# S5 read-out tables of layer 0: formed beside the attention, kept in DRAM, and fetched by the read-out

## The chip, the core and the metric

The kernel runs on one core of a Trainium2 chip, as one launch. The metric is the device time of one execution in microseconds, as the median of several executions. TensorE does the matmuls, VectorE and ScalarE the elementwise work, GpSimd (POOL) the S5 scan and a few stores, and SyncE (SP) issues nearly all DMAs, in order, from one queue.

## The reference, cut to what matters

The model is a two-layer diffusion backbone over 256 latent and 256 context tokens of width 1024. Each layer projects the modulated tokens once and feeds three mixers beside each other, whose results are gated, summed and projected out, followed by an FFN. All matmuls of the projections run as three fp32r products (high and low halves), so their cost is three times a plain one.

The mixer that the change touches is the S5 branch: 32 groups of 16 channels, 64 complex states per group, two directions, a linear recurrence over the tokens.

```python
def s5_readout(x_re, x_im, c_re, c_im):
    return (jnp.einsum('ghp,blgp->blgh', c_re, x_re)
            - jnp.einsum('ghp,blgp->blgh', c_im, x_im))
...
        y_lat = y_lat + seq_order(s5_readout(xl_re, xl_im, c_re[dirn], c_im[dirn]), rev)
...
    g = jax.nn.gelu(y)
    return g * jax.nn.sigmoid(g @ w_glu + b_glu)
```

The kernel does the recurrence over chunks of eight tokens. The states at the chunk edges come from a scan on GpSimd. Inside a chunk each output is the sum of a part from the chunk's own inputs (the direct weights, 8 x 8 taps of 16 x 16) and of a part from the states at its two edges, times C times the powers of the transition (the read-out tables). Tables and direct weights depend on the parameters alone, not on the tokens.

## The kernel before, in words

`layer` strings stages together with `weave(main, (side, rate), ...)`: for each step of the main generator, so many steps of each side generator are issued; what is left of the sides follows at the end. The order on each engine is then written by a planner that runs the whole program in a model of its timeline, so instructions may be taken ahead of others on their engine; the order of the source gives their priority. On the chip each engine, and SyncE's queue, takes its instructions in the order written.

Layer 0 runs these stages around the change: `m_na(l, 0)` (keys, values and queries of half the heads, beside the S5 input side); `m_na(l, 1)` beside `s5_scan` on GpSimd, `attn(l, 0)` and five steps of `ada` (modulation weights of later stages); `gates(l, 0)`, eight projections of 128 gate columns, beside `attn(l, 1)` and `ada`; `gates(l, 2)` beside the S5 read-out `s5_out` and `ada`; then `branch_mm(l, 2)`, the matmuls of the attention branch, and `m_ret` beside `s5_glu`. Each of the attention's halves holds six softmax passes (two head pairs, three passes each).

`s5_out` works through four blocks of eight groups. In layer 0 it forms for each block, in place:

- `s5_g`: fetches C (lines 665 to 667, three DMAs), flips a sign on ScalarE (line 1110), and forms the 128 x 2304 tables `gb` by `_prods`, six products on VectorE of 128 x 1152 (lines 737 to 739, two directions).
- `s5_kwin`: 32 matmuls of the tables with BB, the input-side weights (line 1146), two copies (lines 1150, 1151), three small additions (lines 1152, 1155), and a store of the 128 x 480 direct weights to `kws` in DRAM (line 1159).
- `s5_t`: reads them back as the tile `T`, shifted so that each tap finds its place (four DMAs, line 1133).
- 48 matmuls per token stream, 96 in layer 0 (line 1211), of inputs with `T` and of states with `gb`; then GELU, a transpose and a split (lines 1218 to 1225).

Layer 1 does it otherwise. Its tables and direct weights are formed by `s5_kwins(1)` in the FFN of layer 0, the tables are stored to `gsp` (line 1169), and `s5_out` fetches them by `s5_back` (line 1124 for the tables, line 1133 for `T`), one block ahead of their use.

A weight is fetched by `wraw` (line 373) into one of four slots of 512 KB, then split into a high half by ScalarE (line 383) and a low half by VectorE (line 384), three deep. Lines 389 to 391 are the three products of `mm3`. A projection of 512 tokens by 128 columns has 24 matmuls of 512 columns. Line 517 is `ada`, and lines 1656 and 1659 end a gate projection (tanh, and a store to `tgs` by GpSimd's queue). Scratch buffers come from one pool, `F`, handed out round robin, so that a buffer's memory is taken again after the pool has turned once.

Of the kernel before, what the change touches and what calls it, by code (L numbers as in the profile page):

```python
# [9 lines left out]
F32 = mybir.dt.float32  # L10
# [8 lines left out]
P = 128  # L19
NL = 2  # L20
# [183 lines left out]
def weave(main, *sides):  # L204

    acc = [0.0] * len(sides)
    live = [True] * len(sides)

    def step(i):
        try:  # L210
            next(sides[i][0])
        except StopIteration:
            live[i] = False

    for _ in main:
        for i, (_, each) in enumerate(sides):
            acc[i] += each
            while live[i] and acc[i] >= 1.0:
                acc[i] -= 1.0
                step(i)  # L220
    while any(live):
        for i in range(len(sides)):
            if live[i]:
                step(i)
# [6 lines left out]
def chain(*gens):  # L231
    for g in gens:
        yield from g


class Net:
# [10 lines left out]
    def run(self, stack):  # L247
        tc, nc = self.tc, self.nc
# [4 lines left out]
        dr = stack.enter_context(tc.tile_pool(name="dr", bufs=1, space=DRAM))  # L253
# [3 lines left out]
        self.kws = dr.tile([NL * 4, P, 480], F32, name="kws")  # L257
        self.tgs = dr.tile([24, P, 512], F32, name="tgs")
        self.xsp = dr.tile([P, 4096], F32, name="xsp")
        self.gsp = dr.tile([4, P, 2304], F32, name="gsp")  # L260
        self.F = Arena(fa, NF, "F")
        self.R = Arena(ra, NR, "R")
        F, R = self.F, self.R
# [624 lines left out]
    def layer(self, l):  # L888
        nc, F = self.nc, self.F
        last = l == NL - 1  # L890
        n = self.nt = 256 if last else 512
        self.n0 = 512 - n
        na = [None, None]
        self.yna = self.yslot[0]
        if l == 0:
            self.ug = F.alloc(2048, "ug", top=True)
            mu = self.m_u(l)
            los = []
            for qt in range(1, 4):
                next(mu)  # L900
                self.ada2(0, qt)
                next(mu)
                los += self.modulate(0, 0, [0, 1], self.rb0, 0, range(qt * 2, qt * 2 + 2))
            self.pfree(self.rb0)
            self.s5_prep_small(self.s5in, los[9])
            for _ in mu:
                pass
            with self.tc.issue_after(self.wdma.ins):
                nc.sync.dma_start(self.xsp, self.xb.ap)
            self.xb.free()  # L910
            b2 = self.s5_tables(0)
            ada = self.ada(0, (2, 3, 4, 5))
            self.adas = ada
            self.X = F.alloc(4 * 66 * 16, "X", top=True)
            e_in = chain(*(g for blk in range(4) for g in (self.s5_e(0, b2, blk), self.s5_in(0, blk))))
            weave(self.m_na(l, 0, na), (e_in, 3))
            self.log_gamma(self.s5in[:, 192:208])
            weave(self.m_na(l, 1, na), (self.s5_scan(l), 18), (self.attn(l, 0, na), 4), (self.take(ada, 5), 1))
            weave(self.gates(l, 0, None), (self.attn(l, 1, na), 1.6), (self.take(ada, 5), 0.5))
            self.swap.free()  # L920
            weave(self.gates(l, 2, None), (self.s5_out(l, self.yslot[1]), 2), (self.take(ada, 5), 0.5))
            self.ug.free()
            self.X.free()
            self.m = F.alloc(8 * n, "m", top=True)
            for _ in self.branch_mm(l, 2, None, self.yna, first=True):
                pass
            weave(self.m_ret(l), (self.s5_glu(l, self.yslot[1], self.yslot[0]), 0.8), (self.ret_decay(l), 0.75))
            self.yret = self.yslot[1]
            tg = F.alloc(8 * n, "tg", top=True)
            weave(chain(self.branch_mm(l, 0, None, self.yslot[0]), self.gates(l, 1, tg)), (self.retention(l), 2))  # L930
            self.x_alloc()
            nc.sync.dma_start(self.xb.ap, self.xsp)
            for _ in self.branch_mm(l, 1, tg, self.yret, final=True):
                pass
        else:
            self.norm(l, 0, [2, 3])
            nc.sync.dma_start(self.xsp, self.xb.ap)
            self.xb.free()
            for _ in self.e_left:
                pass  # L940
            for b in self.tabs[l]:
                b.free()
            self.ug = F.alloc(2048, "ug", top=True)
            self.X = F.alloc(4 * 66 * 16, "X", top=True)
            kpre = self.pair([("ws", l, O_NK + m * 128) for m in range(2)])
            for _ in self.m_u(l):
                pass
            weave(self.m_na(l, 0, na, kpre), (chain(*(self.s5_in(l, blk) for blk in range(4)), self.s5_scan(l)), 20))
            ada = self.adas
            weave(self.m_na(l, 1, na), (self.attn(l, 0, na), 2.5))  # L950
            self.yret = self.yslot[1]
            weave(self.m_ret(l), (self.attn(l, 1, na), 1.2), (self.ret_decay(l), 0.75))
            self.swap.free()
            self.m = F.alloc(8 * n, "m", top=True)
            weave(self.branch(l, 2, self.yna, 0), (self.retention(l), 2.5))
            tg = F.alloc(8 * n, "tg", top=True)
            ys5 = self.yslot[0][:, 1024:]
            weave(chain(self.branch(l, 1, self.yret, 1), self.gates(l, 0, tg)),
                  (chain(self.s5_out(l, self.yslot[0]), self.s5_glu(l, self.yslot[0], ys5)), 1))
            self.ug.free()  # L960
            self.X.free()
            self.x_alloc()
            nc.sync.dma_start(self.xb.ap, self.xsp)
            for _ in self.branch_mm(l, 0, tg, ys5, final=True):
                pass
# [151 lines left out]
    def g_view(gb):  # L1117
        return gb.ap.rearrange("p (q r d n) -> p q r d n", q=4, r=2, d=2)

    def s5_back(self, blk):  # L1120

        nc = self.nc
        gb, T = self.F.alloc(2304, "g"), self.F.alloc(1024, "T")
        nc.sync.dma_start(gb.ap, self.gsp[blk])
        self.s5_t(1, blk, T)
        return gb, T

    def s5_t(self, l, blk, T):
# [33 lines left out]
    def s5_kwins(self, l):  # L1162

        nc = self.nc
        for blk in range(4):
            gb, gv = self.s5_g(l, blk)
            yield
            self.s5_kwin(l, blk, gv)
            nc.sync.dma_start(self.gsp[blk], gb.ap)
            gb.free()  # L1170
            yield

    def s5_out(self, l, ysl):
# [6 lines left out]
            return mk(self.X.ap, (r * 132 + d * 67 + st * 33) * 16 + gp, [[16, 32]])  # L1180

        gh, gl = self.halves(ysl)
        back = self.s5_back(0) if last else None
        for blk in range(4):
            if last:
                gb, T = back
                gv = self.g_view(gb)
                back = self.s5_back(blk + 1) if blk < 3 else None
                yield
            else:  # L1190
                gb, gv = self.s5_g(l, blk)
                yield
                self.s5_kwin(l, blk, gv)
                yield
                T = F.alloc(1024, "T")
                self.s5_t(l, blk, T)
                yield
            Tv = T.ap.rearrange("p (q r n) -> p q r n", q=4, r=2)

            n = self.nt  # L1200
# [626 lines left out]
```

## Time and profile before

| | |
|---|---|
| median of three runs | 1575.58 us (1569.61 to 1577.39) |
| the profiled execution | 1571.81 us, span 1570.0 us, mean granted clock 0.979 |
| TensorE busy | 1494.5 us, 95% |
| VectorE busy | 988.2 us, 63% |
| ScalarE busy | 632.2 us, 40% |
| GpSimd busy | 204.2 us, 13% |
| DMA | 245.92 MB, mean 157 GB/s |

The busy shares are means over stages with different limits. A stage is read from its own stretch: how long each engine was busy in it, the clock that TensorE was granted there (1.00 is 2.4 GHz, 0.50 is 1.2 GHz), the mean busy share of the 16 DMA engines and what they moved. In a row of the windows the engines stand in the order PE, PEld (weight loads), VectorE, ScalarE, GpSimd. In a row of the timeline, the bracket at the end is the idle time just before the instruction and what ended it.

### The profile page before, as it was taken

What the parts mean: (1) busy time and instruction counts of PE and PEld (TensorE: products, weight loads), DVE (VectorE), ACT (ScalarE), POOL (GpSimd) and SP (SyncE); (2) the same over time, 40 slices, a digit from 0 to 9 for tenths busy, and PEclk for the clock granted to TensorE, in tenths of its full rate; (3) what the DMA queues carried; (4) which work ended last, traced back from release to release, by engine and by line L of the source; (5) the groups of instructions that cost most, each with busy time, mean ns of one, the idle gap of its engine ahead of it and who ended that gap; (6) DMA issues with size and microseconds to landing.
All of it is one profiled execution on the core that took longest, in us unless ns stands there. A gap on an engine that the chain in (4) does not pass through costs nothing.

```text
span 1570.0 us, 25507 instructions
## 1 busy us (share of the span) xinstructions
PE 1494.5 (95%) x10066; PEld 1270.5 (81%) x10066; DVE 988.2 (63%) x1799; ACT 632.2 (40%) x1139; POOL 204.2 (13%) x541
## 2 busy tenths in 40 slices
PE   7979999969999999999999999999998999999997
PEld 5767677747887888887887788898677999899997
DVE  6784444466446588587699973732654776766566
ACT  4545544223422344332333322544644345443443
POOL 0004983000000000000000000006981000000000
PEclk9989999979999999999999999999999999999999
DMA  9413346654433333454566662422224786655553
GB/s 370 150 61 104 126 141 192 191 160 146 130 103 94 133 95 121 161 187 135 172 220 197 215 192 66 168 102 79 93 91 112 235 298 193 211 176 188 175 186 97
DMA packets 78585, 245.92 MB, mean 157 GB/s; under 512 B 9088, under 2 KB 22912, under 8 KB 76672
## 3 DMA queue, kind: packets, MB, share of 16 engines
q1 hardware_dynamic: 76864, 237.92, 46.3%
q0 software_dynamic: 1600, 6.36, 1.4%
q8 instruction: 79, 1.29, 0.3%
q14 instruction: 42, 0.34, 0.1%
HBM read 225.96 MB, written 16.12 MB: 154 GB/s over the span
## 4 chain that ended last, share of the span: by engine, by line
PE 88%; DMA 4%; DVE 4%; ACT 2%; issue 1%; SPq 0%; POOL 0%; POOLq 0%; DVEq 0%; ACTq 0%
PE psall L389 23%; PE psall L391 22%; PE psall L390 22%; PE psall L862 3%; PE psall L864 3%; PE psall L863 3%; DMA fa<-in_wst_dram 2%; PE psall L1049 1%; PE psall L1363 1%; PE psall L1398 1%; PE psall L1370 1%; PE psall L517 1%; PE psall L1211 1%; PE psall L754 1%; PE psall L1570 1%
## 5 line engine op out<-in xcount | busy, mean ns | idle before, releaser
L389 PE MATMUL psall<-ra 128*128 128x256 f32 (+1 forms) x2122 | 713.7, 341 | 10.5 <-DVE fa L1152 3.7
L391 PE MATMUL psall<-ra 128*128 128x256 f32 (+1 forms) x2122 | 708.9, 337 | 1.8 <-DVE ra L384 1.8
L390 PE MATMUL psall<-ra 128*128 128x256 f32 (+1 forms) x2122 | 710.5, 336 | 0.0
L384 DVE TENSOR_TENSOR ra<-fa,ra 128x1024 fp32r<-128x1024 f32 (+1 forms) x284 | 343.5, 1212 | 297.8 <-ACT ra L383 282.8
L383 ACT CAST ra<-fa 128x1024 fp32r<-128x1024 f32 (+1 forms) x284 | 293.7, 1037 | 564.4 <-PE psall L390 327.7
L389 PEld LDWEIGHTS psall<-ra 128*128 128x128 f32 x2122 | 402.9, 191 | 68.4 <-issue 11.7
L391 PEld LDWEIGHTS psall<-ra 128*128 128x128 f32 x2122 | 405.0, 191 | 45.4 <-issue 3.1
L390 PEld LDWEIGHTS psall<-ra 128*128 128x128 f32 x2122 | 406.0, 191 | 39.5 <-issue 1.1
L1089 POOL TENSOR_TENSOR fa<-fa 128x64 f32<-128x64 f32 x252 | 90.5, 380 | 139.0 <-ACT fa L1057 129.4
L561 DVE SCALAR_TENSOR_TENSOR fa<-fa 128x1024 f32<-128x1024 f32 x70 | 87.6, 1283 | 8.5 <-DMA fa<-in_wst_dram 8.2
L1038 POOL MEMSET fa<- 128x32 f32 x2 | 0.2, 124 | 693.2 <-DVE ra L824 693.2
L862 PE MATMUL psall<-ra 128*128 128x512 f32 x192 | 76.2, 410 | 5.6 <-ACT ra L823 4.8
L863 PE MATMUL psall<-ra 128*128 128x512 f32 x192 | 75.9, 398 | 0.0
L864 PE MATMUL psall<-ra 128*128 128x512 f32 x192 | 72.6, 399 | 0.0
L1694 DVE SCALAR_TENSOR_TENSOR fa<-psall,fa 128x256 f32<-128x256 f32 x96 | 43.3, 482 | 46.4 <-PE psall L391 46.0
L862 PEld LDWEIGHTS psall<-ra 128*128 128x128 f32 x192 | 43.5, 229 | 13.2 <-ACT ra L823 5.8
L1092 POOL TENSOR_TENSOR fa<-fa 128x64 f32<-128x64 f32 x126 | 50.5, 400 | 0.0
L1093 POOL TENSOR_TENSOR fa<-fa 128x64 f32<-128x64 f32 x126 | 48.0, 381 | 9.8
L863 PEld LDWEIGHTS psall<-ra 128*128 128x128 f32 x192 | 43.9, 230 | 4.9
L864 PEld LDWEIGHTS psall<-ra 128*128 128x128 f32 x192 | 42.0, 229 | 5.8 <-issue 0.4
L738 DVE TENSOR_TENSOR fa<-fa 128x1024 f32<-128x1024 f32 (+1 forms) x32 | 40.4, 1288 | 7.4 <-DMA fa<-in_s5c_dram 7.3
L405 ACT CAST ra<-fa 128x512 fp32r<-128x512 f32 (+1 forms) x52 | 26.5, 510 | 41.6 <-DVE fa L1760 29.1
(246 smaller groups left out, 1385.4 us busy)
## 6 DMA issues: line engine op xcount, KB each, us to landing
fa<-in_wst_dram SPq DMA_DIRECT2D x364, 512.0 KB
fa<-in_wst_dram SPq DMA_DIRECT2D x16, 384.0 KB
gsp<-fa SPq DMA_DIRECT2D x4, 1152.0 KB
fa<-gsp SPq DMA_DIRECT2D x4, 1152.0 KB
xsp<-fa SPq DMA_DIRECT2D x2, 2048.0 KB
tgs<-fa POOLq DMA_DIRECT2D x16, 256.0 KB, 4.2
fa<-kws SPq DMA_DIRECT2D x32, 128.0 KB
fa<-tgs SPq DMA_DIRECT2D x16, 256.0 KB
```

What stands on the lines that cost most here:

```text
L383: nc.scalar.copy(hi[:, :n], t[:, :n])
L384: nc.vector.tensor_tensor(out=lo[:, :n], in0=t[:, :n], in1=hi[:, :n].bitcast(F32), op=ALU.subtract)
L389: mm(out, wh, xh, start=start, stop=False)
L390: mm(out, wh, xl, start=False, stop=False)
L391: mm(out, wl, xh, start=False, stop=stop)
L561: nc.vector.scalar_tensor_tensor(out=acc[s].ap, in0=t, scalar=c, in1=acc[s].ap, op0=ALU.mult, op1=ALU.add)
L862: mm(o, xh, hi[:, ws], start=(kk == 0), stop=False)
L863: mm(o, xh, lo[:, ws], start=False, stop=False)
L864: mm(o, xl, hi[:, ws], start=False, stop=(kk == 7))
L1089: e.tensor_tensor(out=t[:, i], in0=at(pf, pr), in1=tab[:, i * 64:(i + 1) * 64].rearrange("p (r d g) -> p r d g", r=2, d=2), op=ALU.mult)
L1092: e.tensor_tensor(out=at(cf, cr), in0=at(cf, cr), in1=t[:, 0], op=ALU.add)
L1093: e.tensor_tensor(out=at(cf, cr), in0=at(cf, cr), in1=mk(T[s % 2], 96, [[-32, 2], [16, 2], [1, 16]]), op=ALU.add)
```

## The change

`s5_kwins(0)` is called in layer 0 too: two of its blocks beside the second half of the projections and the first half of the attention, the other two beside `gates(l, 0)` and the second half of the attention. It forms the tables and direct weights of layer 0 and stores both to DRAM; `gsp` holds both layers' tables, eight blocks in place of four. `s5_out` then takes the same path in both layers: `s5_back` fetches a block's tables (1152 KB) and direct weights, and the next block's fetch is issued before the present block's matmuls. The steps of `s5_out` per block fall from five to three in layer 0.

```diff
-        self.gsp = dr.tile([4, P, 2304], F32, name="gsp")
+        self.gsp = dr.tile([NL * 4, P, 2304], F32, name="gsp")
...
+            kw = self.s5_kwins(0)
...
-            weave(self.m_na(l, 1, na), (self.s5_scan(l), 18), (self.attn(l, 0, na), 4), (self.take(ada, 5), 1))
-            weave(self.gates(l, 0, None), (self.attn(l, 1, na), 1.6), (self.take(ada, 5), 0.5))
+            weave(self.m_na(l, 1, na), (self.s5_scan(l), 18), (self.attn(l, 0, na), 4), (self.take(ada, 5), 1),
+                  (self.take(kw, 4), 1))
+            weave(self.gates(l, 0, None), (self.attn(l, 1, na), 1.6), (self.take(ada, 5), 0.5), (kw, 0.5))
...
-    def s5_back(self, blk):
+    def s5_back(self, l, blk):
...
-        nc.sync.dma_start(gb.ap, self.gsp[blk])
-        self.s5_t(1, blk, T)
+        nc.sync.dma_start(gb.ap, self.gsp[l * 4 + blk])
+        self.s5_t(l, blk, T)
...
-            nc.sync.dma_start(self.gsp[blk], gb.ap)
+            nc.sync.dma_start(self.gsp[l * 4 + blk], gb.ap)
...
-        back = self.s5_back(0) if last else None
+        back = self.s5_back(l, 0)
         for blk in range(4):
-            if last:
-                gb, T = back
-                gv = self.g_view(gb)
-                back = self.s5_back(blk + 1) if blk < 3 else None
-                yield
-            else:
-                gb, gv = self.s5_g(l, blk)
-                yield
-                self.s5_kwin(l, blk, gv)
-                yield
-                T = F.alloc(1024, "T")
-                self.s5_t(l, blk, T)
-                yield
+            gb, T = back
+            gv = self.g_view(gb)
+            back = self.s5_back(l, blk + 1) if blk < 3 else None
+            yield
```

## Rows read from the trace of the kernel before

**Rows 1.** The page's header.
```profile
span 1570.0 us, 25507 instructions
```

**Rows 2.** Windows: us, busy by engine (instructions), PEclk, DMA share, GB/s.
```profile
140.00:200.00 60.00, 53.84 (x361) 38.35 (x360) 30.01 (x73) 29.50 (x80) 53.99 (x155) 1.00 0.41 135
200.00:265.00 65.00, 65.00 (x394) 46.66 (x394) 25.75 (x57) 29.38 (x77) 42.10 (x108) 1.00 0.53 168
265.00:290.00 25.00, 25.00 (x136) 18.08 (x135) 19.49 (x17) 7.95 (x12) 1.62 (x3) 1.00 0.50 170
290.00:331.00 41.00, 40.24 (x418) 30.77 (x415) 16.08 (x20) 11.82 (x20) 2.70 (x5) 1.00 0.66 207
331.00:358.00 27.00, 14.71 (x94) 10.18 (x93) 17.17 (x22) 3.31 (x7) 0.00 (x0) 0.62 0.47 149
358.00:390.00 32.00, 32.00 (x301) 25.77 (x300) 23.21 (x41) 15.32 (x30) 0.00 (x0) 1.00 0.41 119
```

**Rows 3.** Timeline of TensorE, 288 to 362 us: start, duration, line, operation, wait before.
```profile
289.93 1.89 PE L1146 MATMUL psall<-fa 128*32 128x128 f32 x59
...
330.20 0.39 PE L390 MATMUL psall<-ra 128*128 128x512 f32 x1
330.43 0.39 PE L391 MATMUL psall<-ra 128*128 128x512 f32 x1
...
336.95 0.63 PE L1146 MATMUL psall<-fa 128*32 128x128 f32 x2 [5.45 <-DVE fa L739]
339.15 1.95 PE L1146 MATMUL psall<-fa 128*32 128x128 f32 x30 [1.56 <-DVE fa L739]
344.55 0.79 PE L389 MATMUL psall<-ra 128*128 128x512 f32 x1 [3.45 <-DVE fa L1152]
...
356.64 0.63 PE L389 MATMUL psall<-ra 128*128 128x512 f32 x1
357.07 0.57 PE L390 MATMUL psall<-ra 128*128 128x512 f32 x1
```

**Rows 4.** Waits of SyncE's queue, 300 to 360 us: total, times, longest.
```profile
SPq L373 <- DVE ra L384: 8.4, 3, 5.4
SPq L1159 <- DVE fa L1155: 7.7, 2, 7.4
```

**Rows 5.** Timelines of SyncE's queue and of VectorE, 310 to 362 us.
```profile
318.19 8.83 SPq L373 DMA_DIRECT2D fa<-in_wst_dram  x3
...
327.11 0.52 SPq L666 DMA_DIRECT2D fa<-in_s5c_dram  x1
...
332.40 1.36 DVE L738 TENSOR_TENSOR fa<-fa 128x1152 f32<-128x1152 f32 x1 [5.14 <-DMA fa<-in_s5c_dram]
```

**Rows 6.** Groups by line and shape, VectorE, 140 to 290 us.
```profile
L738 DVE TENSOR_TENSOR fa<-fa 128x1152 f32<-128x1152 f32 x4 | 5.2, 1353 | 0.0
```

**Rows 7.** Windows, read-out of layer 1.
```profile
1235.00:1245.00 10.00, 10.00 (x86) 10.00 (x84) 8.47 (x33) 4.38 (x8) 0.00 (x0) 1.00 0.98 314
1245.00:1255.00 10.00, 10.00 (x90) 9.23 (x93) 3.52 (x5) 2.83 (x5) 0.00 (x0) 1.00 0.98 281
...
1265.00:1275.00 10.00, 10.00 (x154) 9.56 (x155) 7.53 (x13) 5.57 (x10) 0.00 (x0) 1.00 0.98 389
```

**Rows 8.** Waits of TensorE, 1225 to 1295 us.
```profile
PE psall L389 <- ACT ra L383: 1.1, 1, 1.1
```

**Rows 9.** Windows, FFN of layer 0, where layer 1's tables are formed.
```profile
840.00:870.00 30.00, 30.00 (x158) 24.11 (x157) 27.97 (x31) 6.24 (x10) 0.00 (x0) 1.00 0.68 222
```

**Rows 10.** DMA issues of the page: operation, count, KB each.
```profile
gsp<-fa SPq DMA_DIRECT2D x4, 1152.0 KB
...
kws<-fa SPq DMA_DIRECT2D x8, 240.0 KB
...
fa<-in_s5c_dram SPq DMA_DIRECT2D x16, 64.0 KB
fa<-in_s5c_dram SPq DMA_DIRECT2D x8, 128.0 KB
```

## The prediction

> **What bounds the kernel now.** I began with the page's span and then cut the part of layer 0 that the edit touches into stretches [rows 1, 2]. The reader should follow two columns there: the first, TensorE's busy time against the length of the stretch, and PEclk, the share of the full 2.4 GHz that was granted. From 200 to 290 us TensorE has no gap. From 290 to 331 it misses 0.8 us. From 331 to 358 it is busy for only 14.7 of 27 us and its clock falls to 0.62. From 358 it is full again. So the kernel is bound by TensorE, except in one hole inside the S5 read-out of layer 0, and smaller ones between 140 and 200 us, where 60.0 - 53.8 = 6.2 us are idle in the first attention half.
>
> The timeline of TensorE says what the hole is [rows 3]. The gate projections run to 331 us. Then the direct-weight matmuls of block 2 (L1146) wait 5.45 us for the products of line 739, the rest of them 1.56 us more, and the next projection 3.45 us for line 1152, which is still the same block's chain (products, matmuls, two copies, an addition). After the gap the matmuls start 0.43 us apart (356.64 to 357.07) where they were 0.23 apart before it (330.20 to 330.43): the lower of the two clock levels, 1.2 GHz. The timeline of VectorE and of SyncE's queue says why the products are late [rows 5]: three weight fetches hold the queue from 318.19 for 8.83 us, the C fetch of block 2 leaves only at 327.11, and VectorE's first product waits 5.14 us for it. The queue's own waits show the same order from the other side [rows 4]: it stood 8.4 us for weight slots, and 7.7 us in front of the store of the direct weights, because that store waits for line 1155.
>
> **The change, part by part.**
>
> *Removed from the read-out.* Four times per layer the C fetch, its sign flip, six products, the direct-weight matmuls with their copies, and the store-then-load of the direct weights through DRAM. None of it is deleted; it goes some 100 us earlier. What the read-out gains is the hole: 27.0 - 14.7 = 12.3 us of idle time [rows 2]. With the gap goes the low clock behind it: 20 matmuls of 512 columns from 344.55 to 357.07 [rows 3], 0.43 - 0.23 = 0.20 us each, make 4.0 us; the 30 direct-weight matmuls at 339.15 took 1.95 us where 59 took 1.89 at 289.93, which makes 1.0 us. Together 5.0 us, so 17.3 us at most come back here, and the stretch would shrink from 27 to 9.7 us. Below it is bounded by zero, if the new fetches arrive as late as the old products (first rival).
>
> *Added to the read-out.* One fetch of 1152 KB of tables per block [rows 10], 4 x 1.18 = 4.72 MB. From 290 to 358 the engines moved 41 x 207 + 27 x 149 GB/s = 12.5 MB [rows 2]. Take off three stores of direct weights (3 x 0.25 MB) and the C fetches of two blocks (2 x 0.26 MB), which both lie there, and 16.0 MB must pass in 68 - 17.3 = 50.7 us: 315 GB/s. The nearest rows are the same fetches in layer 1 [rows 7]: 314 and 281 GB/s at a DMA share of 0.98, then 389 at 0.98 in a stretch of mostly large transfers. At 389 nothing is lost; at 281 the bytes need 56.9 us, 6.2 too many. I take 300, between the two rows that hold table and direct-weight fetches together: 53.3 us, a loss of 2.6, say 3. It is no more because the share is 0.50 just before and 0.41 just after [rows 2], so some of it can slide. TensorE's longest wait in that stretch of layer 1 was a single 1.1 us [rows 8].
>
> The Trainium skill ("DMA: Bandwidth & Descriptors", Specifications) puts the limit of HBM for one core near 358 GB/s. By it the 16.0 MB would take 44.7 us, the 3 us would be zero and the sum 3 us lower. The trace went over it, 389 GB/s in one stretch [rows 7], and under it with full engines in the two others, so I keep the price from the rows.
>
> *Moved beside the attention.* 24 products (six per block) at 1.353 us, 32.5 us of VectorE [rows 6], where VectorE is busy for 30.0 of 60 and 25.8 of 65 us [rows 2]. It would rise to about 88 of 125 us, 0.71. Half of this is only pulled forward a little: the products of the first two blocks ran before 290 already, four on each of the lines 737 to 739 [rows 6], with TensorE at 25.0 of 25.0 [rows 2]. For cover: in the layer-1 FFN, where these same products are formed for layer 1, VectorE is busy for 27.97 of 30 us and TensorE for all 30 [rows 9]. That is a stage of long independent projections; the attention has a chain through VectorE in each of its 12 softmax passes, and VectorE takes its instructions in order, so a softmax row maximum can stand behind a run of products. The bounds are 0 and the whole 32.5. I take 2 us: the 6.2 us already lost in the first half, raised in proportion to VectorE's busy share (0.50 to about 0.70, a factor of 1.4), give 2.5, and the second half loses nothing today.
>
> *Queued behind.* SyncE's queue gets four stores of 1152 KB that wait for line 739, and the stores of the direct weights move to the same place. Behind each stand weight fetches. Today's stores of this kind held the queue for at most 7.4 us, 7.7 in all [rows 4], and TensorE stayed full until 331; four weight slots of 5.4 us of projection each (24 matmuls by 0.23) lie in between. I cost this at nothing beyond the 2 us; without the cover it would be those 7.7 us. The matmuls of the direct weights are the same number in another place. The scratch buffers fit beside the attention's, but the ring of the free pool turns faster, which is part of the 2 us too.
>
> *Sum.* 1571.8 (the profiled execution: span 1570.0 and 1.8 around it) - 17.3 + 3 + 2 = 1559.5, say **1559**. The profiled execution lies 3.8 under the median of the three runs, 1575.6, and inside their range, 1569.6 to 1577.4; I make no correction for that and put it into the range. What comes behind 358 us is bound by TensorE with DMA at 0.41, so it should move forward as a whole.
>
> **The rivals.**
>
> *The read-out still ends late (0.16, same).* The table fetch has to stand in the same queue as the weights, and the queue waits in order: 8.83 us for three weight fetches just ahead of the C fetch that came late [rows 5]. If the tables of two blocks arrive as late as that C fetch (5.14 us of wait each, 10.3 us) and the low clock follows one of the gaps (2.5 us), 12.8 of the 17.3 us are given back; with the 2 us of the attention 1571.8 - 17.3 + 12.8 + 2 = 1569. For it: layer 0 has wider projections and the gate stores on top. Against it: the fetch is issued one block ahead, some 11 us (one and a half gate projections and 2.7 us of read-out), and layer 1 does the same without such a gap [rows 8]. The Trainium skill ("DMA: Bandwidth & Descriptors", Anatomy of one DMA) says that DMA engines do not wait on semaphores; the wait happens on the issuing sequencer, before dispatch. The waits of SyncE's queue agree with it [rows 4].
>
> *The attention becomes the bound (0.10, slower).* If the products stand ahead of the softmax on VectorE and TensorE has nothing else ready, each of 12 passes loses up to two products, 2.7 us: 32.5 us more, 1571.8 - 17.3 + 3 + 32.5 = 1590. It turns into a loss against no change from about (17.3 - 3) / 12 = 1.2 us per pass, and beyond the measurement (below) from (1583.5 - 1571.8 + 17.3 - 3) / 12 = 2.2. For it: TensorE already waits in that half, 6.2 us. Against it: from 200 to 290 it does not wait at all, though the first products are there, and projections and gates stand beside every pass.
>
> *The forecast (0.74, faster),* with every price of the DMA from 0 to 6.2 us and of the attention from 0 to 6 us.
>
> **How the numbers follow.** A measurement of this kernel can tell about 0.5%, 7.9 us, from no change, so faster is below 1567.7 and slower above 1583.5. Lowest: no loss anywhere, 1554.5, less a further 3 for the spread of the runs, 1551. Highest: 6.2 and 6 us lost, 1566.7, and 5.6 us of spread from the profiled execution to the longest run, 1572; this also takes in the first rival. Some 6 in 100 are left below and 14 above. Chances 0.74, 0.16 and 0.10, from the three cases.
>
> **What would show it right or wrong.** Right: between 290 and about 345 us TensorE has no gap over 2 us and its clock stays at 1.00; lines 737 to 739 of layer 0 lie between 140 and 270; DMA share near 0.9 in the read-out; the first matmul of the branch stage follows the last gate projection at once. Wrong in the read-out: matmuls of line 1211 that wait for the gsp or kws fetch, or weight casts that wait for their DMA, with the clock at 0.5. Wrong in the attention: idle time of TensorE between 140 and 265 above 9 us, released by softmax lines. The prediction as a whole fails if the planner's new order opens a gap in a stage that I count as full.

## The result, and the profile after

The changed kernel took 1589.74 us (median of six runs, 1586.08 to 1590.94), the kernel before 1573.37 on the same chip: a ratio of 1.0089, 95% interval 1.0071 to 1.0106. It is slower by 0.9%, and 31 us above the forecast. The profiled execution's header, and its windows over the stretches of [rows 2] and over the two in the FFN of layer 0 of which [rows 9] holds the first:

```profile
span 1588.6 us, 25560 instructions
```

```profile
140.00:200.00 60.00, 51.37 (x346) 35.24 (x345) 39.47 (x72) 26.06 (x71) 54.45 (x124) 0.94 0.40 139
200.00:265.00 65.00, 52.21 (x328) 36.83 (x325) 28.24 (x54) 22.45 (x61) 53.47 (x136) 0.89 0.50 157
265.00:290.00 25.00, 23.41 (x135) 16.22 (x134) 17.91 (x29) 11.21 (x30) 5.52 (x5) 1.00 0.68 252
290.00:331.00 41.00, 41.00 (x409) 31.15 (x411) 15.54 (x26) 14.36 (x26) 2.16 (x4) 1.00 0.82 281
331.00:358.00 27.00, 27.00 (x311) 22.07 (x304) 14.01 (x18) 11.03 (x22) 2.17 (x4) 1.00 0.73 262
358.00:390.00 32.00, 32.00 (x154) 25.75 (x153) 14.88 (x22) 10.75 (x16) 0.54 (x1) 1.00 0.47 162
840.00:870.00 30.00, 30.00 (x171) 23.81 (x170) 28.14 (x31) 9.90 (x14) 0.00 (x0) 1.00 0.70 232
870.00:900.00 30.00, 20.53 (x116) 14.73 (x115) 24.86 (x31) 6.24 (x9) 0.00 (x0) 0.89 0.47 155
```

Read against [rows 2], the read-out did what was forecast: from 290 to 390 us TensorE has no gap and its clock is 1.00 throughout. The loss stands ahead of it, between 140 and 290, and again at 870 to 900. Two milestones of TensorE divide the 18.6 us by which the span grew. The first is the first matmul of the retention branch, which comes after the attention and the read-out (line 1544 before, line 1537 after).

```profile
L1544 PE MATMUL psall<-fa x16: 272/275/276, 461.8 to 463.5; 128*128 128x128 f32 x16
```

```profile
L1537 PE MATMUL psall<-fa x16: 272/275/275, 468.8 to 470.4; 128*128 128x128 f32 x16
```

There the kernel is 7.0 us late, and 1.7 of them it has already where the scan starts (139.09 before, 140.77 after). The rest is the sum of a gain and a loss, each of idle time and of time at the lower clock; in what follows the lower clock counts as half of the time for which TensorE was busy at 1.2 GHz.

- The read-out, 290 to 390: 13.1 us idle before and 0 after, and 12.1 us busy at 1.2 GHz before and none after, which is 6.0. Given back: 19.1 us.
- The attention, 140 to 300: 6.2 us idle before and 23.0 after, and no time at 1.2 GHz before and 15.9 us after, which is 7.9. Lost: 24.7 us.

24.7 - 19.1 + 1.7 makes 7.3, near the 7.0. The second milestone is the end of layer 1's first S5 stage: there the kernel is 17.8 us late (the next projection's second matmul starts at 1083.22 where it started at 1065.39), and 7.6 us of the difference are idle time in the FFN.

**What the attention waits for.** The waits of TensorE from 140 to 300 us, and one of SyncE's queue from 200 to 300:

```profile
PE psall L1363 <- ACT fa L1649: 8.5, 1, 8.5
PE psall L1356 <- ACT fa L1330: 7.4, 2, 3.9
```

```profile
SPq L1373 <- DMA tgs<-fa: 17.8, 1, 17.8
```

Line 1373 fetches the bias of an attention head, line 1652 stores a gate tile to `tgs`, line 1649 makes it. The timelines of ScalarE, GpSimd, SyncE's queue, TensorE and VectorE join these rows:

```profile
208.60 0.59 ACT L1649 ACTIVATE fa<-psall 128x512 f32<-128x512 f32 x1
...
228.82 0.73 POOL L1652 DMA_DIRECT2D tgs<-fa  x1
...
231.27 0.81 SPq L1373 DMA_DIRECT2D fa<-in_nabias_dram  x2
...
233.78 0.94 ACT L1374 ACTIVATE fa<-fa 128x384 f32<-128x384 f32 x2 [17.59 <-DMA fa<-in_nabias_dram]
...
236.19 1.11 PE L1363 MATMUL psall<-fa 128*128 128x128 f32 x4 [8.50 <-ACT fa L1649]
...
246.73 0.60 ACT L1649 ACTIVATE fa<-psall 128x512 f32<-128x512 f32 x1 [8.68 <-DMA tgs<-fa]
...
246.75 1.36 DVE L738 TENSOR_TENSOR fa<-fa 128x1152 f32<-128x1152 f32 x1 [9.85 <-DMA tgs<-fa]
```

The reader should follow one buffer. The gate tile was ready at 209, but its store stands on GpSimd's queue among the instructions of the scan and leaves 20 us later. The pool had handed the tile's memory on to the bias buffer, so the bias fetch waits 17.8 us for that store, with every later weight behind it on SyncE's queue; ScalarE waits 17.59 us for the bias, and TensorE 8.50 for the next thing on ScalarE. In the kernel before, the first store left 1.5 us after its tanh began (188.63, 190.11). The second store does the same to ScalarE and VectorE at 247 us, and the second wait of line 1356 (3.5 us, at 251) follows from it; the first (3.9 us, at 174) is of another kind, a softmax behind a weight that ScalarE awaited for 6.05 us.

The first store stands behind 186 of the scan's 252 instructions. Before the change the scan was that far at 212.6 us; after it, at 228.8.

**Why the scan is late.** Timelines of GpSimd and of VectorE in the changed kernel, about 217 us (lines 1091 to 1095 are the scan; a row x2 holds two instructions):

```profile
216.38 0.39 POOL L1095 TENSOR_TENSOR fa<-fa 128x64 f32<-128x64 f32 x1
216.85 2.79 POOL L1091 TENSOR_TENSOR fa<-fa 128x64 f32<-128x64 f32 x2
219.60 1.43 POOL L1094 TENSOR_TENSOR fa<-fa 128x64 f32<-128x64 f32 x1
221.11 1.32 POOL L1095 TENSOR_TENSOR fa<-fa 128x64 f32<-128x64 f32 x1
...
223.32 0.32 POOL L1094 TENSOR_TENSOR fa<-fa 128x64 f32<-128x64 f32 x1
...
216.51 1.47 DVE L738 TENSOR_TENSOR fa<-fa 128x1152 f32<-128x1152 f32 x1
...
218.10 2.75 DVE L737 TENSOR_TENSOR fa<-fa 128x1152 f32<-128x1152 f32 x2
...
220.85 1.40 DVE L739 TENSOR_TENSOR fa<-fa 128x1152 f32<-128x1152 f32 x1
```

A scan instruction that takes 0.32 us by itself takes 1.3 to 1.4 while a product runs, and ends about when the product ends. Over the whole scan, the largest group of its instructions and the DMA that ends it, before and then after:

```profile
L1089 POOL TENSOR_TENSOR fa<-fa 128x64 f32<-128x64 f32 x126 | 44.5, 374 | 88.6 <-ACT fa L1057 83.8
...
241.20 0.55 POOL L1099 DMA_DIRECT2D fa<-fa  x1 [0.29 <-POOL fa L1093]
```

```profile
L1091 POOL TENSOR_TENSOR fa<-fa 128x64 f32<-128x64 f32 x126 | 55.9, 465 | 87.9 <-ACT fa L1059 83.2
...
257.14 0.56 POOL L1101 DMA_DIRECT2D fa<-fa  x1 [0.30 <-POOL fa L1095]
```

The scan itself is needed only in the read-out. What hurts is what stands in order behind it.

**What the FFN waits for.** TensorE's timeline in the changed kernel, where layer 1's tables are formed:

```profile
877.60 1.19 PE L1148 MATMUL psall<-fa 128*32 128x128 f32 x30 [1.49 <-DVE fa L739]
...
886.77 0.50 PE L389 MATMUL psall<-ra 128*128 128x512 f32 x1 [3.72 <-ACT ra L383]
...
891.68 0.79 PE L391 MATMUL psall<-ra 128*128 128x512 f32 x1 [3.11 <-DVE ra L384]
```

No line here was edited. The pool stood at word 13056 instead of 2304 when the branch stage began, and this stage's buffers lie elsewhere.

### The profile page after: what moved, and what is told of

Its sections match the earlier page's. It is cut to its first block, busy times and chain, and to the rows that moved or that the text cites. A ratio compares the mean times of both kernels' runs of the same rounds, so it can differ in the third digit from the quotient of the medians.

```text
span 1588.6 us, 25560 instructions
## 1 busy us (share of the span) xinstructions
PE 1500.3 (94%) x10066; PEld 1275.0 (80%) x10066; DVE 992.3 (62%) x1799; ACT 632.9 (40%) x1139; POOL 221.3 (14%) x541
## 4 chain that ended last, share of the span: by engine, by line
PE 66%; POOL 13%; issue 11%; DMA 4%; DVE 3%; ACT 1%; SPq 1%; POOLq 0%; DVEq 0%; ACTq 0%
PE psall L389 19%; PE psall L391 19%; PE psall L390 19%; POOL fa L1091 7%; POOL fa L1095 3%; DMA fa<-in_wst_dram 3%; POOL fa L1094 3%; PE psall L1204 1%; PE psall L1563 1%; PE psall L862 1%; PE psall L517 1%; DVE fa L561 1%; PE psall L864 1%; PE psall L863 1%; PE psall L1577 1%
## 5 line engine op out<-in xcount | busy, mean ns | idle before, releaser
L1091 POOL TENSOR_TENSOR fa<-fa 128x64 f32<-128x64 f32 x252 | 104.5, 436 | 137.7 <-ACT fa L1059 128.2
L738 DVE TENSOR_TENSOR fa<-fa 128x1024 f32<-128x1024 f32 (+1 forms) x32 | 42.4, 1338 | 26.6 <-DMA fa<-in_s5c_dram 14.0
L1095 POOL TENSOR_TENSOR fa<-fa 128x64 f32<-128x64 f32 x126 | 53.4, 424 | 9.9
L862 PEld LDWEIGHTS psall<-ra 128*128 128x128 f32 x192 | 43.5, 229 | 12.7 <-ACT ra L823 5.7
L1094 POOL TENSOR_TENSOR fa<-fa 128x64 f32<-128x64 f32 x126 | 47.4, 376 | 0.0
L737 DVE TENSOR_TENSOR fa<-fa 128x1024 f32<-128x1024 f32 (+1 forms) x32 | 40.6, 1304 | 5.2 <-ACT fa L1112 4.3
```

The lines of the kernel that those rows point to most:

```text
L862: mm(o, xh, hi[:, ws], start=(kk == 0), stop=False)
L1091: e.tensor_tensor(out=t[:, i], in0=at(pf, pr), in1=tab[:, i * 64:(i + 1) * 64].rearrange("p (r d g) -> p r d g", r=2, d=2), op=ALU.mult)
L1094: e.tensor_tensor(out=at(cf, cr), in0=at(cf, cr), in1=t[:, 0], op=ALU.add)
L1095: e.tensor_tensor(out=at(cf, cr), in0=at(cf, cr), in1=mk(T[s % 2], 96, [[-32, 2], [16, 2], [1, 16]]), op=ALU.add)
```

## The experiments

Three theories stood against each other. The chain: the slow scan holds up stores on GpSimd's queue and the buffers behind them. The pool: its turned position makes waits where no line changed. The rival of the prediction: VectorE is simply overloaded, and softmax row maxima stand behind products. The expectations name theories by letters as they stood at the time. The table gives TensorE's idle time in three stretches (length less busy time, from the windows), and for the attention also what the lower clock cost (half of TensorE's busy time at 1.2 GHz, from the trace's granted clock). Each ratio is to runs of the kernel before that were made beside it; their medians were 1573.4 for after, 1575.3 for e1 to e4, 1575.9 for e5 to e8 and 1576.7 for e9 to e12, so runs of different groups are compared by their ratios.

| kernel | idle 140-300 | lower clock 140-300 | idle 290-390 | idle 840-910 | median us | ratio to before (95%) |
|---|---|---|---|---|---|---|
| before | 6.2 | 0.0 | 13.1 | 1.8 | 1573.4 | 1 |
| after | 23.0 | 7.9 | 0.0 | 9.5 | 1589.7 | 1.0089 (1.0071 to 1.0106) |
| e1_cursor | 20.8 | 11.0 | 0.0 | 1.7 | 1580.3 | 1.0027 (1.0010 to 1.0044) |
| e2_btop | 18.9 | 7.2 | 0.0 | 0.0 | 1574.0 | 0.9997 (0.9982 to 1.0011) |
| e3_gact | 22.7 | 9.8 | 0.0 | 8.4 | 1588.5 | 1.0077 (1.0052 to 1.0102) |
| e4_load | 12.5 | 6.4 | 3.8 | 5.2 | 1578.4 | 1.0021 (1.0000 to 1.0043) |
| e5_both | 13.8 | 11.6 | 1.7 | 2.4 | 1571.7 | 0.9965 (0.9948 to 0.9982) |
| e6_tab | 16.4 | 14.0 | 0.0 | 2.4 | 1579.9 | 1.0030 (1.0012 to 1.0049) |
| e7_late | 36.0 | 14.2 | 1.1 | 2.6 | 1593.7 | 1.0119 (1.0090 to 1.0148) |
| e8_before | 8.2 | 3.4 | 10.1 | 1.7 | 1572.8 | 0.9979 (0.9963 to 0.9994) |
| e9_top | 11.8 | 3.5 | 0.0 | 2.3 | 1568.7 | 0.9950 (0.9933 to 0.9967) |
| e10_half | 7.9 | 6.4 | 4.1 | 1.7 | 1566.0 | 0.9931 (0.9914 to 0.9948) |
| e11_onein | 15.6 | 5.0 | 0.0 | 8.8 | 1576.2 | 1.0000 (0.9986 to 1.0015) |
| e12_half_top | 11.1 | 3.2 | 0.0 | 3.0 | 1564.2 | 0.9928 (0.9906 to 0.9950) |

**e1_cursor: the pool alone.** After, with the pool's position put back to that of the kernel before, ahead of the branch stage of layer 0.

```diff
+            F.cursor = 2304
             self.m = F.alloc(8 * n, "m", top=True)
```

> The changed kernel, with the scratch pool's cursor set back after the read-out to where it stands at that point in the kernel before, so that every scratch buffer from there on lies where it lay before. Theory A (the attention loses because the pool hands out memory that a gate tile still holds, and the FFN of layer 0 loses because its buffers lie otherwise): the gap between 876 and 892 us in the FFN goes, the hole between 220 and 256 stays; 8 to 10 us less than the changed kernel, near 1580. Theory B (VectorE's products themselves delay softmax and scan): the same for the attention; the FFN is not explained by it, so no gain is needed, near 1589. Theory C (the planner's order after the edit is by chance worse): no change, near 1589.

Windows of it:

```profile
140.00:300.00 160.00, 139.22 (x879) 97.03 (x879) 90.26 (x166) 62.87 (x168) 113.13 (x262) 0.91 0.52 177
...
840.00:910.00 70.00, 68.28 (x399) 53.28 (x399) 67.66 (x79) 22.23 (x31) 0.00 (x0) 1.00 0.68 230
```

The gap in the FFN is gone (1.7 us, as before the change) and the time is 0.6% lower, some 10 us; the attention is as bad as in after (20.8 us idle and 11.0 of the lower clock, 31.8 where after has 30.9). In every later run with the position put back this stretch idles for 1.7 to 3.0 us. So the second loss is a matter of where buffers lie, and of the order that the planner makes of it; no work was taken out.

**e2_btop: the bias buffer alone.** After, with the bias buffers of layer 0 taken from the pool's other end.

```diff
-                bias.append(F.alloc(384, "bias"))
+                bias.append(F.alloc(384, "bias", top=l == 0))
```

> The changed kernel, with layer 0's attention bias buffers taken from the top end of the scratch pool in place of the turning ring, so that a bias fetch never takes the memory of a gate tile. Theory A: SyncE's queue no longer stands 17.8 us in front of the bias fetch, the hole at 220 to 256 us shrinks by 8 us or more, near 1579. Theory B: the products and the slow scan are unchanged, at most 3 us less, near 1587.

The wait of the bias fetch for the store falls from 17.8 to 2.8 us, and the whole loss of the change is gone, more than its expectation had (1579). But most of it went in the FFN, whose gap this move of buffers happens to close; in the attention 18.9 us stay idle, because another buffer got the gate tile's memory (waits of ScalarE and of TensorE, 140 to 300 us):

```profile
ACT fa L1387 <- DMA tgs<-fa: 12.7, 1, 12.7
```

```profile
PE psall L1391 <- ACT fa L1387: 8.1, 1, 8.1
```

**e3_gact: the stores off GpSimd's queue.** After, with the gate stores issued by ScalarE.

```diff
-                self.nc.gpsimd.dma_start(self.tgs[gi * 8 + mt], t.ap)
+                self.nc.scalar.dma_start(self.tgs[gi * 8 + mt], t.ap)
```

> The changed kernel, with the stores of the gate tiles issued by ScalarE's queue in place of GpSimd's, where they stood behind the scan; buffers and products unchanged. Theory A: gate tiles are stored within a few us of their tanh, nothing waits on them, the hole at 220 to 256 us goes: 10 to 14 us less than the changed kernel, 1576 to 1580, and with the FFN's gap still there. The scan stays slow (about 257 us for its end) and this costs nothing. Theory B: the scan and the softmax are as slow as before, at most 3 us less, near 1587.

No gain, where 10 to 14 us were expected: 22.7 us idle in the attention. The timelines of ScalarE and TensorE show a second engine in order behind the scan:

```profile
253.09 0.63 ACT L1076 ACTIVATE fa<-fa 128x32 f32<-128x32 f32 x4 [19.79 <-POOL fa L1091]
```

```profile
255.20 0.80 PE L389 MATMUL psall<-ra 128*128 128x512 f32 x1 [13.35 <-ACT fa L1649]
```

Line 1076 prepares the scan factors of layer 1. The planner had pulled it up into layer 0, into memory that layer 0's scan must leave first; ScalarE stands 19.8 us in front of it, with the gates behind. A theory of the store alone falls here.

**e6_tab, e5_both, e8_before: both things behind the scan.** All three hold line 1076 back to layer 1 (in the expectations, "the run above" and "the first run" are e5_both). e6_tab is after with that and e1_cursor's edit; e5_both also takes e3_gact's edit; e8_before is the kernel before with the held line and the moved stores, as a control.

```diff
-                nc.scalar.activation(hi, tmp.ap, AF.Identity, bias=sh)
+                self.after_mod = nc.scalar.activation(hi, tmp.ap, AF.Identity, bias=sh).ins
...
+        with self.tc.issue_after(self.after_mod) if l else nullcontext():
```

> As the run above, but the gate stores stay on GpSimd's queue: only the ScalarE instructions for layer 1's scan table are moved. Theory D: gate tiles are still stored 20 us late, and what takes their memory still waits; 6 to 10 us of the hole stay: 1574 to 1579. Theory A: 1577 to 1580. If ScalarE's table instructions were the whole cause, 1568.

> The changed kernel with the pool's cursor set back after the read-out (as in the first experiment), and with both things that stand behind the scan taken away: the gate stores issued by ScalarE's queue, and the four ScalarE instructions that prepare layer 1's scan table, which must wait until layer 0's scan has left the scratch, kept behind layer 1's first norm. Theory D (the products slow GpSimd's scan, and engines stand in order behind instructions that wait for its end): the hole between 220 and 256 us goes, idle time of TensorE from 140 to 300 us falls from 23 to 10 us or less, the scan still ends late; 1566 to 1570. Theory A (only memory reuse): the hole stays because bias fetches still wait for reused buffers, 1577 to 1580. Theory C (the planner's order by chance): anything, without the hole moving with these two instructions.

> The kernel before with the same two edits as the first run of this call (gate stores by ScalarE's queue, scan table of layer 1 behind its norm), without the change. Theory D: in the kernel before nothing waited long on the scan (3.0 us of ScalarE), so the read-out's hole sets the time as before: 1570 to 1576, no difference. If it is 8 us or more faster, the two edits are a gain of their own and what the first run gains is not due to the change.

Holding the line alone is not enough (e6_tab, at 1579.9 just outside its 1574 to 1579: ScalarE still waits 8.2 us for a gate store, SyncE's queue 11.4). With both, the hole at 220 to 260 us is gone: TensorE is busy there for 40.0 of 40 us, where after has 12.5 us idle. The scan is not faster for it: the instruction that is line 1091 in after takes 486 ns on average there, 465 in after. It only no longer holds anything up. Still, e5_both missed what was expected of it (10 us idle or less, 1566 to 1570): 13.8 us stay idle in the attention and the lower clock costs 11.6, so of the 30.9 us of after 25.4 are left. The control shows that the two repairs by themselves bring the kernel before 0.2%, so at this point the change itself was worth 1.1 us (1572.8 to 1571.7), which the intervals do not separate from nothing. What remains in e5_both shows the prediction's own rival, in VectorE's and TensorE's timelines:

```profile
165.36 1.34 DVE L738 TENSOR_TENSOR fa<-fa 128x1152 f32<-128x1152 f32 x1
166.63 1.28 DVE L1327 TENSOR_REDUCE fa<-psall 128x2 f32<-128x512 f32 x2
167.82 1.34 DVE L739 TENSOR_TENSOR fa<-fa 128x1152 f32<-128x1152 f32 x1
169.09 0.41 DVE L1312 TENSOR_REDUCE fa<-psall 128x1 f32<-128x256 f32 x1
...
172.42 0.47 DVE L1313 CUSTOM_DVE_ANT_0 fa<-psall,fa 128x256 f32<-128x256 f32 x1
```

```profile
169.56 1.65 PE L1358 MATMUL psall<-ra 64*128 64x512 f32 x3 [3.10 <-DVE fa L1312]
```

The row maximum of line 1312 stands behind a run of products and holds TensorE for 3.1 us, and the granted clock is 0.50 from 168.7 to 182.3 us, which costs 6.3 (half of 12.6 us busy). That is the mechanism the prediction named and gave 0.10, but at one pass and not at twelve, and with the lower clock dearer than the wait.

**e4_load: the load without the change.** The kernel before, with 24 products of the same size beside the attention whose results nothing uses, in one buffer of their own (the function that makes them is left out here).

```diff
+            kw = self.s5_load(0)
...
+                  (self.take(kw, 4), 1))
+            weave(self.gates(l, 0, None), (self.attn(l, 1, na), 1.6), (self.take(ada, 5), 0.5), (kw, 0.5))
```

> The kernel before, with 24 more products of the same size on VectorE, given out beside the attention as in the change, into one buffer that nobody reads: VectorE's load without the DMAs, the stores and the pool's turning. The output is the reference's. Theory A: the scan's instructions slow down beside the products, the read-out's hole stays as before, and the attention loses at most 4 us: 1573 to 1577. Theory B: the attention loses what it loses in the changed kernel, 14 to 17 us of idle time between 150 and 300 us: 1587 to 1590.

6.3 us more are idle in the attention and the lower clock costs 6.4, and against the expectation the read-out's hole shrinks from 13.1 to 3.8. So the 3.1 us by which the time rises are not the price of the load. It is also a weak test: with nothing to wait for, the unused products ran from 113 to 155 us, 17 of the 24 before the scan began at 139, and the scan ended at 245.8 (241.2 before). The seven others stood among the first softmax passes, and TensorE's longest wait there, 4.7 us at 150, is for a softmax line (1342). VectorE's load without the chain is thus not nothing, and how much of the 24.7 us it makes stays open.

**e7_late: the products after the scan.** After with e1_cursor's edit, the products beside the gates alone, and tied to the scan's end (the tie held for 20 of the 24).

```diff
-                  (self.take(kw, 4), 1))
-            weave(..., (kw, 0.5))
+            weave(..., (kw, 1))
...
+        if l == 0:
+            self.nc.gpsimd.tensor_copy(gb.ap[:, 0:8], self.X.ap[:, 1040:1048])
```

> The changed kernel with the cursor set back, and the products of layer 0 bound to start after the scan (a small copy on GpSimd from the scan's last state into the table buffer stands ahead of them), all four blocks beside the second half of the attention. Theory D: the scan ends at 240 us as in the kernel before, its instructions keep 0.3 us, the hole between 220 and 256 us goes, and the read-out starts in time: 1565 to 1570. Theory B (VectorE's load on the softmax): the products now lie where few softmax passes are left, also a gain, but the scan plays no part in it: the rows of the scan tell the two apart. If the planner expects the scan's end too early, VectorE itself stands in front of the first product, and there is no gain: 1578 or more.

The scan keeps its pace (line 1091: 370 ns), and the kernel has the highest median of all (the execution in the table's first columns, 1600.0 us, is the longest of its four). VectorE stands 20.0 us in front of the first tied product until the scan is done and its states are moved, with the attention behind it; TensorE's timeline:

```profile
262.00 1.96 PE L1150 MATMUL psall<-fa 128*32 128x128 f32 x32 [18.46 <-DVE fa L739]
```

A free scan is worth nothing when another engine stands in order behind its end.

**e11_onein: the products with one input.** After, with the three lines of a product exchanged for layer 0, so that it leaves out the multiplication by the powers; the first of them (cut):

```diff
-            eng.tensor_tensor(out=o, in0=mk(P2, po, pd), in1=mk(A, wo, wd), op=ALU.mult)
+            eng.tensor_scalar(out=o, in0=mk(A, wo, wd), scalar1=1.0, scalar2=None, op0=ALU.mult)
```

> After, with the 24 products of layer 0 replaced by as many VectorE instructions of the same size with one input in SBUF in place of two (a copy with a factor 1.0); the tables and direct weights of layer 0 are then not those of the reference, and the order of instructions is nearly that of after. If the scan on GpSimd is slowed by the two inputs of the products: line 1091 falls from 465 to about 374 ns and the scan ends near 242 us, as before the change; then the stores behind it leave earlier, the hole at 222 to 256 us shrinks to a few us, and the time to about 1580 (the 10 us in the FFN remain). If it is slowed by any busy VectorE: 440 to 470 ns, the scan ends at 255 or later, the hole stays and the time is 1587 to 1590.

The group of the scan and its end:

```profile
L1091 POOL TENSOR_TENSOR fa<-fa 128x64 f32<-128x64 f32 x126 | 47.3, 396 | 87.7 <-ACT fa L1059 83.0
...
244.44 0.56 POOL L1101 DMA_DIRECT2D fa<-fa  x1 [0.30 <-POOL fa L1095]
```

The scan ends 12.7 us earlier than in after, the wait of the bias fetch falls from 17.8 to 4.7 us, the stretch 220 to 260 has 3.2 us idle where it had 12.5, and the time is back at that of before although the FFN still loses 8.8 us. The first three gate stores stand behind 192, 220 and 235 instructions of the scan, where after has 186, 220 and 236: the order did not move them, the scan came to them earlier. So the scan's pace makes the hole, as the chain says. VectorE has less to do as well (the 24 instructions take 21.6 us in place of 35.0), so this run alone does not tell the scan from VectorE's load; e5_both does, where the load and the slow scan stay and the hole goes. It does not settle the number of inputs either: most of these instructions took 0.74 to 0.95 us where the products took 1.34 to 1.50, and they slowed the scan too, only for a shorter time (last section).

**e9_top, e10_half, e12_half_top: towards a faster kernel.** e5_both with e2_btop's edit; with all four blocks beside the gates and the second half of the attention, not tied to the scan; and with both.

```diff
-                  (self.take(kw, 4), 1))
-            weave(..., (kw, 0.5))
+            weave(..., (kw, 1))
```

> The kernel e5_both (after, with the pool's cursor put back, the gate stores on ScalarE and layer 1's scan factors held back), and also the bias buffers of layer 0 taken from the pool's top. e5_both still lost 13.8 us of TensorE in 140 to 300 us. Theory D (engines in order behind what waits for the slow scan; buffers that turn into waits for a transfer): with the gate stores off GpSimd the bias buffer no longer waits for a store that stands behind the scan, so the edit has nothing left to mend: 1570 to 1573, idle in 140 to 300 again 10 to 14 us, half of it at 160 to 170 (softmax maxima behind products) and half near 285. Rival R (what is left near 285 is also a buffer of the pool that comes free late): moving the bias buffers changes which buffer meets which, the 4 us near 285 go, 1566 to 1569.

> e5_both with all four blocks of products beside the gates and the second half of the attention, none beside the first half. Theory E (part of the loss is the rival that the prediction named, softmax row maxima standing behind products on VectorE, 3.9 us at 160 to 172 us in e5_both): TensorE's idle time in 140 to 180 falls from 7.8 us to the 4 to 5 us of the kernel before, and the time by 3 to 4 us, to 1568, if the second half takes twelve more products without a new gap. Theory D: the scan is then slowed by the same products later on, and what stands behind it moves as well; the time stays at 1571 to 1574, and the loss is found in 220 to 300 us.

> Both edits of e9_top and e10_half on e5_both. Theory D with E: idle in 140 to 300 us of 8 to 10 us, as the kernel before with the same repairs had, and with the read-out full the time is 1562 to 1567, that is, some 8 us (0.5%) below before. Rival O (the place of each wait is set by an order written against times that do not hold on the chip, so that each mended wait gives another one further on): 1570 to 1575, no better than e5_both, with a new gap of 4 us or more somewhere in 140 to 300 or in the FFN at 840 to 910 us.

e10_half did as theory E says: idle time from 140 to 180 falls from 7.8 to 5.6 us, in all of 140 to 300 from 13.8 to 7.9 (the 4.1 us wait near 285 is gone too), the cost of the lower clock from 11.6 to 6.4, and the ratio from 0.9965 to 0.9931, some 5 us. So much of what e5_both still lost in the attention came from where the products stood, not from the queue behind the scan, which stayed slow (its end at 259.5). e9_top came out at rival R's time, but not in its way: the 4.1 us wait near 285 is gone and one of 6.0 us stands at 263, and less is idle at 160. e12_half_top is the fastest, 0.72% below before (0.50 to 0.94), and about 0.5% below the control (0.9928 / 0.9979 = 0.9949, from two sets of runs and so without an interval). Its windows:

```profile
140.00:300.00 160.00, 148.95 (x1063) 106.73 (x1063) 93.62 (x169) 67.26 (x173) 117.53 (x250) 0.98 0.60 203
290.00:390.00 100.00, 100.00 (x812) 80.17 (x812) 50.95 (x75) 36.50 (x60) 0.00 (x0) 1.00 0.66 220
840.00:910.00 70.00, 67.04 (x348) 52.58 (x348) 66.76 (x77) 17.93 (x23) 0.00 (x0) 0.98 0.63 203
```

The read-out is full and the attention has 4.9 us more idle time than before, so the change's idea does pay once nothing stands behind the scan. A wait of 4.3 us is left, for the direct weights that the read-out fetches; e12_half_top and e10_half cannot be told apart by their times.

## Why the prediction was wrong, point by point

**Right: the read-out.** *What the read-out gains is the hole* held: all of the idle time and the lower clock are gone, 13.1 and 6.0 us where the forecast had 12.3 and 5.0, in every version of the change but three, which idle for 4.1 (e10_half), 1.7 (e5_both) and 1.1 us (e7_late) there. The 3 us for crowded transfers came out as zero: the fetches passed at a DMA share of 0.82 with TensorE full. The first rival, a late read-out, did not appear.

**Wrong: "I take 2 us" for the attention.** It measured 24.7 us, 16.8 of them idle time and 7.9 the lower clock behind the gaps, to which the 2 us gave nothing although the same prediction had priced it in the read-out. The working priced the products on VectorE alone, in proportion to its busy share. It left out what they do to GpSimd: the scan, which the prediction does not mention, ended 15.9 us later, and 12.5 of the 16.8 us lie in the hole behind it. The cover it leaned on, the stretch of [rows 9], which lies in layer 0's FFN and not in layer 1's, could not show this: GpSimd is busy there for 0.00 us, and beside the attention for 54.0 of 60 and 42.1 of 65 [rows 2]. The rule stands in the Trainium skill ("SBUF — State Buffer", Who interferes with whom): a VectorE instruction with two SBUF inputs contends with a GpSimd instruction that reads SBUF. The trace agrees: 1.15 us for a scan instruction beside a product, 0.32 without. The prediction's own sign came, over 9 us idle between 140 and 265: it measured 21.4, but softmax lines released only 9.9 of them.

**Wrong: "I cost this at nothing" for what is queued behind.** That step looked at stores on SyncE's queue. The wait came from a store of the gates on GpSimd's queue, through the ring of the pool, to a fetch on SyncE's: 17.8 us, shown by the timelines and by e2_btop, e3_gact and e5_both together. The text did say that the ring turns faster and put it into the 2 us. It should have asked which buffer would follow which.

**Wrong: what comes behind 358 us "should move forward as a whole".** The FFN of layer 0 lost 9.5 us where it had lost 1.8, with a clock of 0.89, and e1_cursor gives it back by one number. The prediction's last sentence names this failure (a gap in a stage counted as full), but no price was put on it.

**The slower rival** was given 0.10 at 1590, beside a measured 1589.7. The number agrees, the mechanism hardly: twelve passes were to lose 2.7 us each behind products; e5_both shows one such wait of 3.1 us, and e4_load one of 4.7. Of the 24.4 us more that were idle (16.8 in the attention, 7.6 in the FFN) 12.5 are the hole behind the scan and 7.6 the pool. That the time came out at 1589.7 is luck for this rival.

**Open.** Every edit makes the planner write a new order for all engines, so no run changes one thing alone; the chain rests on the rows of its waits, not on times. How the attention's loss divides between the chain and softmax behind products is not settled beyond the hole. Why exactly the pool's position opens the FFN gap was followed only to waits for weights and for the previous block's products, not to one buffer. And e9_top's new wait of 6.0 us was not traced further.

## What to carry to other kernels

Before moving elementwise work beside another stage, list not only what VectorE does there but what GpSimd does, and which stores, fetches and early-placed instructions stand in order behind GpSimd's long chain; an engine with 87% of slack in the page can still set the time through its queue. Where scratch memory goes round a ring, a change of what is allocated in one stage can cost as much in a stage 500 us later as it gains here, so try the ring's position by itself before judging the idea. Give a gap of TensorE the price of the lower clock behind it as well: in e5_both a wait of 3.1 us came with 6.3 us of it. When a change is slower, look whether the predicted gain is there: here it was, in full, and three repairs far from the edit and a later start of the products turned +0.9% into -0.7%.

## What the runs showed of the hardware

GpSimd's pace follows what VectorE reads beside it. Mean time of one scan instruction (128x64), sorted by the VectorE instruction that overlaps it the most and for at least half of its time; worked out from the single instructions of both engines in the traces, over the whole scan, with the number of scan instructions in brackets:

| VectorE instruction beside it | before | after | e11_onein |
|---|---|---|---|
| none | 0.322 us (129) | 0.323 (127) | 0.323 (127) |
| product, 128x1152, two inputs in SBUF | | 1.152 (23) | |
| scaled copy, 128x1152, one input in SBUF | | | 0.710 (21) |
| low half of a weight, 128x1024, two inputs in SBUF | 1.040 (12) | 1.167 (8) | 1.038 (11) |
| scaling, 128x512, one input in SBUF | 0.451 (17) | 0.419 (13) | 0.437 (15) |
| row maximum, 128x256, input in PSUM | 0.319 (12) | 0.325 (12) | 0.319 (11) |
| addition, 128x512, one of two inputs in PSUM | 0.318 (6) | 0.324 (8) | 0.323 (7) |

Beside instructions that read PSUM the scan keeps its pace; beside these four that read only SBUF it is slowed, the scaled copies with one input included. The low halves slowed it before the change too. All 252 instructions of the scan take 92.3 us before and 108.7 after, 16.4 more, about the 15.9 by which it ended late; the 23 beside products make 23 x (1.152 - 0.323) = 19.1, less some 2 us because fewer met a low half.

VectorE can be held as well: in after, the product at 268.16 us ran into a GpSimd copy of 64x2112 that had begun 0.45 us earlier and took 1.95, and the product took 2.71 us where the others took 1.34 to 1.50.
